# RWKV pairs: value gathers ahead of the key transposes, and most conditioning sums moved beside the first five pairs

## The chip, the core and the metric

The kernel runs on one core of a Trainium2 chip. TensorE (PE) does matmuls and loads its weights in parallel with them (PEld); VectorE (DVE), ScalarE (ACT) and GpSimd (POOL) do elementwise work; SyncE (SP) issues most DMAs, ACT a few. Each engine works through its own instructions strictly in the order that the program fixed, and waits where an operand or a buffer is not there yet. The metric is device time in microseconds (us).

## The reference

Two transformer-like blocks follow each other. Of the first, this case touches the RWKV-7 mixer (16 heads of 64 channels, 256 context and 512 latent tokens, two directions) and the conditioning vectors:

```
shift, scale, gate = split(silu(c) @ w_ada + b_ada, 3)        # 2048 -> 3 * 2048
def step(state, inp):                                         # per head, both directions
    sa = -einsum('bhvk,bhk->bhv', state, kk_t)
    state = state * w_t + sa * b_t + v_t * k_t
    return state, einsum('bhvk,bhk->bhv', state, r_t)
y = groupnorm(o) * gn_g + gn_b; y = (y + bonus) * silu(z)
x = x + gate * (concat([ya, yb]) @ w_out)                     # then rmsnorm, then block two
shift2, scale2, gate2 = split(silu(c_2) @ w_ada_2 + b_ada_2, 3)
```

The scan is computed in chunks of 64 tokens: within a chunk by small triangular solves and matmuls, from chunk to chunk by a chain of states.

## The kernel before

The part that matters lies between 1240 and 2460 us. The 16 heads go two at a time: `for p in range(npairs)` runs eight **pairs** (0 to 7). Each pair does, in this order in the code:

- `rwkv_rest`: Gram matrices `Gr` and the copy `R`, transposes of the keys (`rpt` to `bk`), gathers of values and of A (`rpv`, `rat` to `UV`), products `rgv` to `GS`, and the bonus;
- `rwkv_lanes`: a triangular solve on DVE, 60 dependent operations on `rL` and `rT` (lines 745 and 746) between transposes; here called the **lane solve**;
- `rwkv_keys(p + 1)`: the next pair's decays, keys and Gram matrices `Ga`;
- `rwkv_levels`: the rest of the inverse (`rpy`, `rpx`, `rmx`), alternating PE, ACT and DVE;
- `rwkv_chain`: the **chain** of 12 chunk states. One step is `pU` on PE, `UV` on ACT, `pU` again, and one DVE multiply `GS<-pU,WC` (L1214), 11 of them in a pair;
- `rwkv_out`: group norm, transposes and the gate `z` (tiles `rosq`, `rzt`), stored to `y_scr`.

Beside the pairs run two kinds of filling work. The **projection** `rwkv_proj(p + 2)` makes r, k, v, z of a later pair: 192 matmuls of 128x512 (`mm`, L394) into the PSUM ring `mm[0]` of two buffers, mixed on their way out in a ring `mix` of two SBUF buffers. `Stream` spreads these matmuls over the steps of a pair. After the last projection, the section under `fill out` does the same with the first part of the output projection: it loads 13 tiles `yf` (in `mix`), splits them, and runs 16 groups of 39 matmuls (L1320), each leaving through a tile `pe` (in `mix`).

The **conditioning sums** are `ada_cols`: for 6144 output columns, each `sum over k of cact[k] * w_ada[k]` runs on DVE as a running sum, 16 steps for each block of columns, in tiles `awt` that are loaded one by one:

```
wt = wts(k); SY.dma_start(wt, wsrc(k))
V.scalar_tensor_tensor(wt, wt, cvec[:, k:k + 1], acc, op0=OP.mult, op1=OP.add)
acc = wt
```

At the end of a block, matmuls with a column of ones add over the partitions into a PSUM tile `pm`. Before the change all 12 blocks of 512 columns (192 steps) stand under `fill out`, in a ring of six `awt` buffers. `early = ()` keeps the loop that would place blocks of 256 columns beside the pairs empty.

Two things set the order. A pool's ring hands out buffers in the order of the code: a tile waits until the tile that had its buffer before is released. And a scheduler orders each engine's instructions from its own estimates, with the pairs at high priority, `Stream` and `Beside` as earliest points; this order is then fixed in the program.

Of the kernel before, what the change touches and what calls it, by code (L numbers as in the profile page):

```python
# [10 lines left out]
FT = mybir.dt.float32  # L11
FR = mybir.dt.float32r
AF = mybir.ActivationFunctionType
# [5 lines left out]
P = 128  # L19
D = 2048  # L20
KT = 16
NX = 512
# [182 lines left out]
def build(tc, a, dbg=None):  # L205
# [3 lines left out]
    PE, V, S, G, SY = nc.tensor, nc.vector, nc.scalar, nc.gpsimd, nc.sync  # L209
    root = ExitStack()  # L210
    with root:
# [17 lines left out]
        ident = cc("ident", P)  # L229
# [23 lines left out]
        mm = [actx.enter_context(tile_pool(name="mps", bufs=2, space=PSUM))]  # L253
# [193 lines left out]
        for i in range(4):  # L447
            px, pc = lx[i], lc[i // 2][:, i % 2]
            m = vc("mu", 24 + i)
# [53 lines left out]
        for d in range(2):  # L503
# [7 lines left out]
            Gr, raw = rows[:, 0], rows[:, 1]  # L511
# [417 lines left out]
        def pg_(shape, name):  # L929
            return gps.tile(shape, FT, name=name, tag="g", bufs=2)  # L930
# [40 lines left out]
        def rwkv_out(p, s):  # L971
            mark(f"r{p} out")
            po, bv = s["po"], s["bv"]
            oa = rp.tile([P, NX], FT, name="oa").rearrange("p (m h t) -> p m h t", m=4, h=2)
            oa8 = oa.rearrange("p m h t -> p (m h) t")
            po8 = po.rearrange("p m h t -> p (m h) t")
            mean = rp.tile([P, 8], FT, name="gmean")
            var = rp.tile([P, 8], FT, name="gvar")
            osq = rp.tile([P, NX], FT, name="rosq").rearrange("p (m t) -> p m t", m=8)
            bc8 = lambda t: t.rearrange("p (j o) -> p j o", o=1).to_broadcast([P, 8, 64])  # L980
            V.tensor_reduce(mean, po8, axis=AX.X, op=OP.add)
            V.tensor_scalar(mean, mean, 1.0 / 64, None, op0=OP.mult)
            V.tensor_tensor(oa8, po8, bc8(mean), op=OP.subtract)
            S.activation(osq, oa8, AF.Square)
            V.tensor_reduce(var, osq, axis=AX.X, op=OP.add)
            zt = rp.tile([P, NX], FT, name="rzt", tag="rosq")
            SY.dma_start(zt, mix_scr["z"][p])
            V.tensor_scalar(var, var, 1.0 / 64, 64e-5, op0=OP.mult, op1=OP.add)
            rsqrt_pow(var, var, 8)
            V.tensor_tensor(oa8, oa8, bc8(var), op=OP.mult)  # L990
            pt = cps.tile([P, 4, P], FT, name="rpto", tag="pU")
            for m in range(4):
                PE.transpose(pt[:, m, :], oa[:, m].rearrange("p h t -> p (h t)"), ident)
            yt = oa.rearrange("p m h t -> p (m h t)")
            S.activation(yt, pt.rearrange("p m t -> p (m t)"), AF.Identity, scale=vc("gn", p), bias=vc("gn", 8 + p))
            G.tensor_tensor(yt, yt, bv, op=OP.add)
            G.tensor_tensor(yt, yt, zt, op=OP.mult)
            S.dma_start(y_scr[8 + p], yt)
# [92 lines left out]
        def rwkv_rest(p, s):  # L1091
# [3 lines left out]
            Gr = [rp.tile([P, 8, 2, 64], FT, name="Gr", bufs=2) for d in dirs]  # L1095
            bk = [rp.tile([P, NC, P], FT, name="bk", bufs=2) for d in dirs]
            R = [rp.tile([P, 2, 8, 64], FT, name="R", bufs=2) for d in dirs]
            for d in dirs:
                gram(p, d, Gr[d], BK[d], A[d][:, NC:], 4, 8, ccr(f"rm{d}")[:, 64:])
                for h, hp_ in enumerate(halves):  # L1100
                    S.activation(R[d][64:, h], A[d][hp_, NC:], AF.Copy)
                for c0 in range(0, NC, 4):
                    pt = pg_([P, 4, P], "rpt")
                    for c in range(4):
                        PE.transpose(pt[:, c, :], BK[d][:, c0 + c, :, :].rearrange("p j t -> p (j t)"), ident)
                    S.activation(bk[d][:, c0:c0 + 4, :], pt, AF.Copy)

            UV = rp.tile([P, NC, 2, 2, 64], FT, name="UV")

# [3 lines left out]
            for d in dirs:  # L1113
# [14 lines left out]
                for c0 in range(0, NC, 4):  # L1128
                    i0 = step_chunk[d].index(c0 + (3 if d else 0))
                    pt = gps.tile([P, 4, P], FT, name="rat", tag="l")  # L1130
                    for c in range(4):
                        PE.transpose(pt[0:64, c, :], A[d][:, c0 + c], ident)
                    S.activation(UV[0:64, c0:c0 + 4, d].rearrange("p c h t -> p c (h t)"), pt[0:64], AF.Copy)
                    pt = gps.tile([P, 4, 2, 64], FT, name="rgv", tag="l")
                    for i in range(4):
                        for h in range(2):
                            PE.matmul(pt[halves[h], i, h, :], Ga[64:, d, step_chunk[d][i0 + i], h], UV[64:, i0 + i, d, h, :], start=True, stop=True, skip_group_check=True)
                    for h, hp_ in enumerate(halves):
                        S.activation(GS[0:64, i0:i0 + 4, d, h], pt[hp_, :, h], AF.Copy)

            V.scalar_tensor_tensor(ksum, rr, vc("r_k", p), ksum, op0=OP.mult, op1=OP.mult)
            pb = pg_([P, NX], "rbo")
# [135 lines left out]
                return tc.issue_after(states[min(i, len(states) - 1)])  # L1278

        start = []  # L1280
        early = ()
        for p in range(1, min(2, npairs)):
            rwkv_proj(p, r0, False, pace, tag="mix", bufs=2)
        with tc.high_priority(offset=4000):
# [1 line left out]
        for p in range(npairs):  # L1286
# [8 lines left out]
                now = nxt  # L1295
            beside = Beside()
            for i in range(early[p] if p < len(early) else 0):
                ada_cols(256 * (sum(early[:p]) + i), 256, lambda k: rp.tile([P, 256], FT, name="awt", bufs=4), gps, "l", beside)
            if p + 2 < npairs:
                stream.n = min(stream.n, start[p])  # L1300
                rwkv_proj(p + 2, r0, False, stream, tag="mix", bufs=2)
# [485 lines left out]
```

## Time and profile before

| | |
|---|---|
| time, median of 3 runs | 3392.07 us (3390.76 to 3399.92) |
| the profiled execution: its time, its span | 3378.85 us, 3377.1 us |
| PE, PEld busy | 3093.9 us (92%), 2447.9 us (72%) |
| DVE busy | 2324.4 us (69%) |
| ACT, POOL busy | 1303.7 us (39%), 952.6 us (28%) |
| granted TensorE clock, mean share of full | 0.924 |

Busy shares are means over stages of different limits: matmuls overlap and their ends are modelled, so a PE at 92% is not at its peak, and a DVE at 69% can be the bound of a stage. In rows of instructions the columns are start and duration in us, engine, line, operation, tiles (written <- read) and, in brackets, the engine's idle time just before and what ended it.

### The profile page before, as it was taken

The page shows a single profiled execution, that of the slowest core. Times are in us where ns is not written, and L with a number is a line of the kernel's source. Part 1 is how long each engine was busy: PE and PEld are TensorE (multiplying, and loading weights), DVE is VectorE, ACT ScalarE, POOL GpSimd, SP SyncE. Part 2 cuts the span into 40 slices and gives each one's busy share as a digit, 9 for nine tenths or more (in the row PEclk, how much of TensorE's full clock was granted, in tenths as well). Part 3 has the DMA queues.
Part 4 walks back from the last instruction along what each step waited for, and adds up shares of the span by engine and source line. Part 5 has one row for each costly group of instructions (what it writes and reads, how often), then busy time and mean ns, then how long its engine had stood idle before and what let it go on. Part 6 is the DMA issues. An engine that isn't in the chain of part 4 may idle for free.

```text
span 3377.1 us, 53576 instructions
## 1 busy us (share of the span) xinstructions
PE 3093.9 (92%) x20464; PEld 2447.9 (72%) x20464; DVE 2324.4 (69%) x3996; ACT 1303.7 (39%) x2767; POOL 952.6 (28%) x794
## 2 busy tenths in 40 slices
PE   7798998999898989999999998989978999999996
PEld 4477887788776867677677776667656778877775
DVE  7977678776887254755646637797678997573577
ACT  5133443344333234435344342413233336573423
POOL 3644343344343232233223232523041000002001
PEclk9899999998999877999999978788989999999998
DMA  8522222222222221212112112568653322223764
GB/s 338 190 76 79 79 70 65 71 84 72 67 65 83 90 70 48 64 49 79 56 59 61 51 55 95 180 186 253 197 198 134 114 84 88 85 79 119 261 212 137
DMA packets 206265, 375.13 MB, mean 111 GB/s; under 512 B 21911, under 2 KB 52280, under 8 KB 202680
## 3 DMA queue, kind: packets, MB, share of 16 engines
q1 hardware_dynamic: 196384, 356.07, 32.9%
q10 hardware_dynamic: 9624, 15.64, 1.3%
q8 instruction: 160, 2.62, 0.3%
q14 instruction: 97, 0.79, 0.1%
HBM read 333.75 MB, written 37.88 MB: 110 GB/s over the span
## 4 chain that ended last, share of the span: by engine, by line
PE 55%; DVE 27%; issue 6%; DMA 3%; ACT 2%; POOL 1%; SPq 0%; DVEq 0%; POOLq 0%; ACTq 0%
PE mm L394 24%; PE po L1758 4%; PE mm L1477 4%; DVE L L746 3%; DVE DG L745 3%; PE rpg L1065 3%; DVE awt L1254 2%; DVE rT L745 2%; DVE rL L746 2%; PE pU L93 2%; DVE acc L587 2%; DMA awt<-in_w_ada 2%; DVE uc L1496 2%; PE mm L1320 2%; PE pl L1016 1%
## 5 line engine op out<-in xcount | busy, mean ns | idle before, releaser
L275 POOL TENSOR_TENSOR w_l<-w_f,w_h 128x512 fp32r<-128x512 f32 x380 | 535.8, 1412 | 1036.7 <-ACT w_h L274 962.3
L274 ACT ACTIVATE w_h<-w_f 128x512 fp32r<-128x512 f32 (+2 forms) x688 | 424.4, 618 | 785.4 <-PE mm L394 265.8
L394 PE MATMUL mm<-hxh,w_l 128*128 128x512 f32 x1472 | 621.5, 422 | 15.5 <-POOL w_l L275 10.0
L394 PE MATMUL mm<-hxh,w_h 128*128 128x512 f32 x1472 | 623.0, 423 | 11.9 <-ACT w_h L274 10.7
L394 PE MATMUL mm<-hxl,w_h 128*128 128x512 f32 x1472 | 606.8, 413 | 0.0
L394 PEld LDWEIGHTS mm<-hxh,w_l 128*128 128x128 f32 x1472 | 290.6, 197 | 77.8 <-POOL w_l L275 12.6
L394 PEld LDWEIGHTS mm<-hxh,w_h 128*128 128x128 f32 x1472 | 288.9, 196 | 74.2 <-ACT w_h L274 13.5
L394 PEld LDWEIGHTS mm<-hxl,w_h 128*128 128x128 f32 x1472 | 289.7, 197 | 61.0 <-issue 1.5
L275 DVE TENSOR_TENSOR w_l<-w_f,w_h 128x512 fp32r<-128x512 f32 (+2 forms) x308 | 219.4, 715 | 145.8 <-ACT w_h L274 144.0
L1254 DVE SCALAR_TENSOR_TENSOR awt<-awt,cacts 128x512 f32<-128x512 f32 x180 | 169.3, 940 | 30.0 <-DMA awt<-in_w_ada 19.6
L1496 DVE SCALAR_TENSOR_TENSOR uc<-up,vecs,uc 128x512 f32<-128x512 f32 x240 | 169.4, 747 | 2.2 <-ACT uc L1494 1.0
L394 PE MATMUL mm<-hch,w_l 128*128 128x256 f32 x512 | 153.9, 301 | 1.4 <-POOL w_l L275 1.3
L394 PE MATMUL mm<-hch,w_h 128*128 128x256 f32 x512 | 150.4, 294 | 0.0
L1065 PEld LDWEIGHTS rpg<-A,BK 64*128 64x128 f32 x1280 | 128.6, 217 | 27.7 <-issue 11.4
L394 PE MATMUL mm<-hcl,w_h 128*128 128x256 f32 x512 | 148.3, 290 | 0.0
L1065 PE MATMUL rpg<-A,BK 64*128 64x64 f32 x1280 | 138.1, 307 | 10.5 <-POOL BK L1051 6.8
L745 DVE TENSOR_TENSOR DG<-L 128x30 f32<-128x30 f32 (+14 forms) x240 | 135.2, 563 | 5.3
L746 DVE TENSOR_TENSOR L<-L,DG 128x30 f32<-128x30 f32 (+14 forms) x240 | 134.1, 559 | 5.4
L745 DVE TENSOR_TENSOR rT<-rL 128x30 f32<-128x30 f32 (+14 forms) x240 | 124.4, 518 | 6.7
L1203 ACT ACTIVATE UV<-pU 64x256 f32<-64x256 f32 x96 | 36.2, 377 | 235.0 <-PE pU L1201 223.9
L236 POOL TENSOR_TENSOR cv<-cv,mh 128x4 f32<-128x4 f32 x1 | 1.4, 1435 | 437.5 <-DVE cv L1564 437.5
L746 DVE TENSOR_TENSOR rL<-rL,rT 128x30 f32<-128x30 f32 (+14 forms) x240 | 117.2, 489 | 6.7
(483 smaller groups left out, 6749.3 us busy)
## 6 DMA issues: line engine op xcount, KB each, us to landing
w_f<-in_w_in SPq DMA_DIRECT2D x496, 256.0 KB, 3.0
awt<-in_w_ada SPq DMA_DIRECT2D x192, 256.0 KB, 3.5
wt<-in_w_ada_t SPq DMA_DIRECT2D x20, 1024.0 KB, 6.5
w_f<-in_w_out SPq DMA_DIRECT2D x80, 256.0 KB, 2.9
awt<-in_w_ada_g SPq DMA_DIRECT2D x64, 256.0 KB, 3.6
wk<-in_w_ada_s SPq DMA_DIRECT2D x16, 768.0 KB, 6.0
w_f<-in_w_out_a SPq DMA_DIRECT2D x48, 256.0 KB, 3.6
lth<-lora_scr SPq DMA_DIRECT2D x32, 288.0 KB, 3.1
```

What stands on the lines that cost most here:

```text
L93: i = self.tc.nc.tensor.matmul(out, lhsT, rhs, start=first is None, stop=True, skip_group_check=True)
L274: S.activation(wh, raw, AF.Copy)
L275: lower[0].tensor_tensor(wl, raw, wh, op=OP.subtract)
L394: PE.matmul(po[:, :n], w_[:, k, :], h_, start=(kt == 0 and i == 0), stop=(kt == KT - 1 and i == 2))
L587: V.scalar_tensor_tensor(acc[:, :n], raw[:, j:j + n], cw(j), acc[:, :n], op0=OP.mult, op1=OP.add)
L745: V.tensor_tensor(t, U[:, r, k:k + 1].to_broadcast([n, k, nc_]), U[:, k:k + 1, c].to_broadcast([n, k, nc_]), op=OP.mult)
L746: step = V.tensor_tensor(U[:, r, c], U[:, r, c], t, op=OP.add)
L1065: ticks[p, d, "gram"] = PE.matmul(pg[h][:, c], BK[hp_, c0 + c, :, :], cols[hp_, c], start=True, stop=True, skip_group_check=True).ins
L1254: V.scalar_tensor_tensor(wt, wt, cvec[:, k:k + 1], acc, op0=OP.mult, op1=OP.add)
L1477: PE.matmul(po, w_[:, k, :], h_[kt], start=(kt == 0 and j == 0), stop=(kt == KT - 1 and j == 2))
L1496: V.scalar_tensor_tensor(uc[t], up[:, j:j + NX], cw(j), uc[t], op0=OP.mult, op1=OP.add)
L1758: PE.matmul(po[t], y_[kt][:, cols], w_, start=(kt == 0 and i == 0), stop=(kt == KT - 1 and i == 2))
```

## The change

Four edits. In `rwkv_rest` the Gram matrices, `R` and the key transposes move behind the gathers. The tiles `rosq` and `rzt` of `rwkv_out` move from a buffer of their own into the ring `mix`. `early` becomes `(4, 4, 4, 4, 4)`: 20 blocks of 256 columns (320 steps, five sixths of the columns) move beside pairs 0 to 4, and 2 of the 12 blocks of 512 stay in the fill (`n_early` becomes 10). Those 20 blocks use two `awt` buffers, and their `pm` tiles come from the ring `mm[0]`.

```
-            osq = rp.tile([P, NX], FT, name="rosq").rearrange("p (m t) -> p m t", m=8)
+            osq = r0.tile([P, NX], FT, name="rosq", tag="mix", bufs=2).rearrange("p (m t) -> p m t", m=8)
...
-            zt = rp.tile([P, NX], FT, name="rzt", tag="rosq")
+            zt = r0.tile([P, NX], FT, name="rzt", tag="mix", bufs=2)
...
-            for d in dirs:
-                gram(p, d, Gr[d], BK[d], A[d][:, NC:], 4, 8, ccr(f"rm{d}")[:, 64:])
...
+            for d in dirs:
+                for c0 in range(0, NC, 4):
+                    pt = pg_([P, 4, P], "rpt")
...
+            for d in dirs:
+                gram(p, d, Gr[d], BK[d], A[d][:, NC:], 4, 8, ccr(f"rm{d}")[:, 64:])
+                for h, hp_ in enumerate(halves):
+                    S.activation(R[d][64:, h], A[d][hp_, NC:], AF.Copy)
...
-        early = ()
+        early = (4, 4, 4, 4, 4)
...
-                ada_cols(256 * (sum(early[:p]) + i), 256, lambda k: rp.tile([P, 256], FT, name="awt", bufs=4), gps, "l", beside)
+                ada_cols(256 * (sum(early[:p]) + i), 256, lambda k: rp.tile([P, 256], FT, name="awt", bufs=2), mm[0], "mm", beside)
```

How the fixed order changes, at three places. First VectorE in the chain of pair 3, from its second to its seventh state multiply (`GS<-pU,WC`); before:

```order
L1214 TENSOR_TENSOR GS<-pU,WC 64x256
L1046 SCALAR_TENSOR_TENSOR BK<-lth,k2r 128x12x64
L1039 SCALAR_TENSOR_TENSOR A<-kmix,vecs_r,E 128x12x63
L1214 TENSOR_TENSOR GS<-pU,WC 64x256 x4
L1141 SCALAR_TENSOR_TENSOR ksum<-rmix,vecs_r,ksum 128x512
L1067 TENSOR_TENSOR Ga<-rpg,consts_r 128x8x64 x2
L1080 STREAM_TRANSPOSE rL<-Ga 32x1024 x2
L1067 TENSOR_TENSOR Ga<-rpg,consts_r 128x4x64
L1214 TENSOR_TENSOR GS<-pU,WC 64x256
```

and of the change, in the same chain:

```order
L1215 TENSOR_TENSOR GS<-pU,WC 64x256
L1255 SCALAR_TENSOR_TENSOR awt<-awt,cacts 128x256 x3
L1215 TENSOR_TENSOR GS<-pU,WC 64x256
L1255 SCALAR_TENSOR_TENSOR awt<-awt,cacts 128x256 x2
L425 SCALAR_TENSOR_TENSOR mr<-mm,vecs,mr 128x8x63
L1255 SCALAR_TENSOR_TENSOR awt<-awt,cacts 128x256
L1215 TENSOR_TENSOR GS<-pU,WC 64x256
L1255 SCALAR_TENSOR_TENSOR awt<-awt,cacts 128x256 x3
L1215 TENSOR_TENSOR GS<-pU,WC 64x256
```

Up to three steps of the sums now stand between two multiplies of the chain, and the next pair's lane solve (`rL<-Ga`), which began inside this chain, now begins behind it. From pair 0's second multiply to pair 5's first, all 320 steps stand in VectorE's order: 52 inside the lane solves of pairs 2 to 5 (14, 12, 12, 14), 36 between the ends of these solves and the first multiplies of their chains (8, 10, 10, 8), and 232 elsewhere.

Second TensorE in the chain of pair 7, with output-projection matmuls (`mm`) between the two halves of a step; before:

```order
L1201 MATMUL pU<-GS,Ga 64x64 x4
L1320 MATMUL mm<-hxh_20586,w_h 128x512
L1320 MATMUL mm<-hxh_20586,w_l 128x512
L1320 MATMUL mm<-hxl_20587,w_h 128x512
L1320 MATMUL mm<-hxh_20592,w_h 128x512
L1320 MATMUL mm<-hxh_20592,w_l 128x512
L1320 MATMUL mm<-hxl_20593,w_h 128x512
L1320 MATMUL mm<-hxh_20598,w_h 128x512
L1320 MATMUL mm<-hxh_20598,w_l 128x512
L93 MATMUL pU<-GS,consts 64x256
L93 MATMUL pU<-UV,bk 64x64 x4
```

and of the change, the end of that chain (`rpo` is the output of pair 7, `rpto` its last transposes):

```order
L93 MATMUL pU<-GS,consts 64x256
L93 MATMUL pU<-UV,bk 64x64 x4
L93 MATMUL rpo<-UV,Gr 64x64 x4
L1202 MATMUL pU<-GS,Ga 64x64 x4
L93 MATMUL rpo<-GS,R 64x64 x4
L93 MATMUL rpo<-UV,Gr 64x64 x4
L1321 MATMUL mm<-hxh_21626,w_h 128x512
L1321 MATMUL mm<-hxh_21626,w_l 128x512
L993 MATMUL rpto<-consts,oa 128x128 x4
L1321 MATMUL mm<-hxl_21627,w_h 128x512
```

All 624 matmuls of the partial output projection now stand behind pair 7's last chain step; pairs 6 and 7 have none beside them. Likewise the chains of pairs 0 and 1 have no projection matmuls beside them; the 192 of one projection stand in one block behind chain 1, and those of the others stand in the chains of pairs 2 to 5, some 24 to a step instead of 7 (240 within the ten steps of chain 5).

Third ScalarE, which issues the loads of `yf`, around pair 6's output (`rosq`) before:

```order
L1106 ACTIVATE bk<-rpt 128x512 x3
L1306 DMA yf<-y_scr 128x512
L984 ACTIVATE rosq<-oa 128x512
L1306 DMA yf<-y_scr 128x512
L1309 ACTIVATE hxh_20586<-yf 128x512
```

and in the change around pair 7's, behind the eleven last copies of its chain:

```order
L1204 ACTIVATE UV<-pU 64x256 x11
L984 ACTIVATE rosq<-oa 128x512
L1307 DMA yf<-y_scr 128x512
L1310 ACTIVATE hxh_21626<-yf 128x512
L1307 DMA yf<-y_scr 128x512
L995 ACTIVATE oa<-rpto,vecs_r 128x512
```

The first load of `yf` moved from beside pair 6's end to pair 7's end, since `rosq` and `rzt` of pair 7 now stand ahead of `yf` in the ring `mix`.

## Rows read from the trace of the kernel before

**Rows 1.** Windows by stage: start:end, us, busy by engine, clock, DMA share, GB/s.

```profile
1238.00:1352.80 114.80, 105.28 (x865) 81.39 (x865) 65.90 (x115) 42.44 (x80) 23.99 (x17) 0.70 0.13 38
...
1617.80:1755.10 137.30, 130.43 (x1182) 97.47 (x1181) 81.23 (x133) 56.70 (x106) 41.53 (x30) 0.95 0.20 61
...
2098.00:2304.00 206.00, 176.69 (x1326) 138.85 (x1325) 171.97 (x242) 69.67 (x133) 76.88 (x52) 0.78 0.62 194
2304.00:2461.50 157.50, 147.34 (x1202) 113.06 (x1200) 100.80 (x143) 48.07 (x98) 29.67 (x23) 0.99 0.72 227
2461.50:3377.00 915.50, 849.73 (x3738) 671.59 (x3738) 664.04 (x1039) 383.15 (x761) 92.13 (x70) 0.96 0.42 136
```

**Rows 2.** Groups by form: the sums' step in the fill; a like one of 256 columns.

```profile
L1254 DVE SCALAR_TENSOR_TENSOR awt<-awt,cacts 128x512 f32<-128x512 f32 x180 | 169.3, 940 | 30.0 <-DMA awt<-in_w_ada 19.6 <-DMA awt<-in_w_ada_g 7.0
...
L957 DVE SCALAR_TENSOR_TENSOR k2r<-kmix,vecs_r,rpb 128x256 f32<-128x256 f32 x8 | 3.8, 472 | 4.4 <-PE rpb L955 4.4
```

**Rows 3.** DMA issues, 1490 to 2030 us: tiles, queue, count, size, median us to landing.

```profile
w_f<-in_w_in SPq DMA_DIRECT2D x60, 256.0 KB, 3.3
...
rzt<-mix_z SPq DMA_DIRECT2D x4, 256.0 KB, 2.6
...
wup<-in_w_up SPq DMA_DIRECT2D x8, 48.0 KB, 1.9
```

**Rows 4.** Timeline of DVE and SP: a result, then its store.

```profile
2098.00 0.67 DVE L839 SCALAR_TENSOR_TENSOR mz<-mzth,mm 128x512 f32<-128x512 f32 x1
...
2098.70 0.33 SPq L844 DMA_DIRECT2D mix_z<-mz  x1
```

**Rows 5.** The chain of waits, then DVE's timeline: a load and the step behind it.

```profile
2280.43 4.56 DMA awt<-in_w_ada
...
2285.08 1.20 DVE L1254 SCALAR_TENSOR_TENSOR awt<-awt,cacts 128x512 f32<-128x512 f32 x1 [0.47 <-DMA awt<-in_w_ada]
```

**Rows 6.** Timeline of DVE, late stage: the sums of block two, four buffers.

```profile
3202.31 0.75 DVE L1712 SCALAR_TENSOR_TENSOR awt<-awt,cacts 128x512 f32<-128x512 f32 x1 [0.69 <-DMA awt<-in_w_ada]
3203.85 0.75 DVE L1712 SCALAR_TENSOR_TENSOR awt<-awt,cacts 128x512 f32<-128x512 f32 x1 [0.79 <-DMA awt<-in_w_ada]
```

**Rows 7.** Chain multiplies of pairs 0, 5, 7: durations, first and last start.

```profile
L1214 DVE TENSOR_TENSOR GS<-pU,WC x11: 427/427/428, 1323.2 to 1385.7; 64x256 f32<-64x256 f32 x11
...
L1214 DVE TENSOR_TENSOR GS<-pU,WC x11: 427/428/428, 2024.1 to 2088.5; 64x256 f32<-64x256 f32 x11
...
L1214 DVE TENSOR_TENSOR GS<-pU,WC x11: 427/428/428, 2375.4 to 2433.9; 64x256 f32<-64x256 f32 x11
```

**Rows 8.** Timeline of DVE: two multiplies of chain 7, no `mm` between.

```profile
2402.20 0.43 DVE L1214 TENSOR_TENSOR GS<-pU,WC 64x256 f32<-64x256 f32 x1 [1.11 <-PE pU L93]
...
2405.18 0.43 DVE L1214 TENSOR_TENSOR GS<-pU,WC 64x256 f32<-64x256 f32 x1 [0.51 <-PE pU L93]
```

**Rows 9.** Lane solve of pair 0: first transposes, then the end mark.

```profile
L1080 DVE STREAM_TRANSPOSE rL<-Ga x4: 1889/1896/1899, 1238.0 to 1244.5; 32x1024 f32<-32x1024 f32 x4
L749 DVE MEMSET rL<- x1: 85/85/85, 1276.2 to 1276.2; 128x32 f32 x1
```

**Rows 10.** The chain of waits: matmuls in a row; Gram matmuls of a direction.

```profile
1484.63 1.93 PE rpg L1065 x32
...
2440.15 8.63 PE mm L1320 x36
```

**Rows 11.** Timeline of PE: projection matmuls that start 0.42 us apart.

```profile
1198.28 0.63 PE L394 MATMUL mm<-hxh,w_h 128*128 128x512 f32 x1
1198.70 0.63 PE L394 MATMUL mm<-hxh,w_l 128*128 128x512 f32 x1
```

**Rows 12.** Tile `yf`, 2098 to 2461 us; then PE's first `po` behind the fill.

```profile
L1309 ACT ACTIVATE hxh<-yf x14: 619/631/634, 2103.2 to 2460.9; 128x512 fp32r<-128x512 f32 x14
L1310 POOL TENSOR_TENSOR hxl<-yf,hxh x13: 1266/1708/2777, 2103.9 to 2155.1; 128x512 fp32r<-128x512 f32 x13
...
DMA to landing us min/median/max: 3.0/4.7/6.1
...
2462.46 0.91 PE L1320 MATMUL po<-hxh,w_h 128*128 128x512 f32 x2 [3.34 <-ACT w_h L274]
```

More of the change, by code (lines that the diff above doesn't have):

```diff
@@ L1097, in rwkv_rest @@
             R = [rp.tile([P, 2, 8, 64], FT, name="R", bufs=2) for d in dirs]
-            for d in dirs:
-                gram(p, d, Gr[d], BK[d], A[d][:, NC:], 4, 8, ccr(f"rm{d}")[:, 64:])
[L1100 to L1106, printed above, removed]
             UV = rp.tile([P, NC, 2, 2, 64], FT, name="UV")
@@ L1139, in rwkv_rest @@
                         S.activation(GS[0:64, i0:i0 + 4, d, h], pt[hp_, :, h], AF.Copy)
+            for d in dirs:
+                for c0 in range(0, NC, 4):
+                    pt = pg_([P, 4, P], "rpt")
+                    for c in range(4):
+                        PE.transpose(pt[:, c, :], BK[d][:, c0 + c, :, :].rearrange("p j t -> p (j t)"), ident)
+                    S.activation(bk[d][:, c0:c0 + 4, :], pt, AF.Copy)
+            for d in dirs:
+                gram(p, d, Gr[d], BK[d], A[d][:, NC:], 4, 8, ccr(f"rm{d}")[:, 64:])
+                for h, hp_ in enumerate(halves):
+                    S.activation(R[d][64:, h], A[d][hp_, NC:], AF.Copy)
             V.scalar_tensor_tensor(ksum, rr, vc("r_k", p), ksum, op0=OP.mult, op1=OP.mult)
```

## The prediction

> **What bounds the kernel now.** Read first the windows by stage [rows 1]. One period of the steady pairs (1617.8 to 1755.1) takes 137 us; PE is busy for 130 of it, VectorE (DVE) for 81. So DVE has some 56 us without work in each period. In the fill (2098 to 2461.5) it is the other way: DVE is busy for 273 of 363 us, and 169 of them are the sums' steps [rows 1, 2]. These steps also made DVE wait 30 us, most of it for their own loads. So moving sums from the fill to the pairs moves them to where DVE has room. Whether they can use it depends on what a step waits for, and there the reader should look at the loads, not at DVE.
>
> A step needs its load, and a load needs a free buffer. Block two's sums (far behind, with four buffers) already show steps that DVE waits for: 0.69 and 0.79 us idle ahead of steps 1.54 us apart, each ended by a load [rows 6].
>
> The fixed order decides the rest: every engine takes its instructions in the order shown above, late or not.
>
> **The round trip with two buffers.** Step k reads its own tile and that of step k-1. With two buffers the load for step k+1 takes the buffer of tile k-1, and that is free only when step k has ended. So no load is ever in flight while its predecessor's step still waits: step, issue, load, step, one after the other. The price of one round:
>
> - the step: the trace has no such step of 256 columns; a like operation of that size took 0.472 us [rows 2];
> - step to issue: a result of DVE at 2098.67 let SP issue at 2098.70, 0.03 us [rows 4];
> - the load of 128 KB: between 1.9 us (48 KB) and 2.6 us (256 KB, `rzt`) in the quiet pairs, with 3.3 us for the crowded `w_f` as the far end [rows 3]. I take 2.3, the middle of the first two, since half the loads run while few others do;
> - landing to step: a load issued at 2280.43 took 4.56 us, its step began at 2285.08, 0.09 us later [rows 5].
>
> Sum 2.9 us, bounds 2.5 to 3.9. DVE works for 0.47 of it; 320 rounds are 928 us, but five periods of 137 us are only 685. A period would have to last 64 x 2.9 = 186 us. DVE's room is not what limits.
>
> **First term: from pair 0's first chain multiply to pair 5's.** Before: 1323.2 to 2024.1 [rows 7]. After, by what stands in DVE's order:
>
> - 52 steps inside four lane solves. A solve takes 38.2 us alone [rows 9]; 13 steps between its operations add 13 x 0.47 = 6, and their round trips hide behind five operations each. Four times 44 is 176;
> - 36 steps between a solve's end and its chain. Pair 0 took 47 us there [rows 7, 9], with 33 matmuls of 0.24 us (36 in 8.63 us [rows 10]) that are gone. Nine rounds are 26. I take 35, bounds 26 and 47: four times 35 is 140;
> - the other 232 steps at 2.9: 673. A chain step alone takes 2.98 us [rows 8], so two or three steps between two multiplies set its length, and even 24 projection matmuls beside it (24 x 0.24 + 2.98 = 8.7) only equal three rounds.
>
> Together 989. The start moves forward a little, as 60 projection matmuls (14 us) leave the order ahead of it: taken as 8, so 1315. The end is 2304, **280 us later** than before.
>
> **Second term: the fill that stands behind pair 7.** Before, from pair 5's first multiply to PE's first `po` matmul, 438 us (2024.1 to 2462.5) [rows 7, 12]. After, from the order:
>
> - chain 5 with 240 projection matmuls: 10 x 2.98 + 240 x 0.24 = 88;
> - pair 5's output, 96 more matmuls (23 us) and Gram matrices: 30;
> - pair 6's solve with its last transposes: 41;
> - to its chain: 32 steps of 512 columns at 0.94 [rows 2] and some 34 other DVE operations at 0.43: 45;
> - chain 6, with four to nine operations of the next pair in a step: 10 x 5 = 50; the 39 operations left of pair 7's solve at 0.5: 20;
> - pair 7's levels 35, its chain 10 x 2.98 = 30, its output 5;
> - the 13 loads of `yf` through two buffers: load 4.7, copy 0.63, subtraction 1.71 [rows 12], so 7.0 x 13 / 2 = 46 until the first group can end (bounds 33, with the fastest load and subtraction, and 58);
> - 15 more groups of 39 matmuls at 0.24: 140.
>
> Together 530, **92 us more**. Before, most of these 624 matmuls (150 us of PE) lay between the steps of pairs 6 and 7. The cause is the ring `mix`: `yf` and `pe` now follow pair 7's `rosq` and `rzt` in it. The same ring and the `pm` tiles in `mm[0]` hold each projection back until the sums ahead of it are done; that lies inside the first term, where the sums end last.
>
> **Third term: PE's clock.** Beside pair 0, PE was granted 0.70 of full speed on average, against 0.95 in the steady pairs [rows 1]; in the slow stretches matmuls start 0.42 us apart [rows 11] and not 0.24, so at 1.2 GHz in place of 2.4. PE will have more idle time, with 137 us of the same work in a period of some 190. If a sixth of the six projections' 1152 matmuls run slow, that is 192 x 0.18 = **35 us**; none gives 0, all give 207. On this the Trainium skill speaks against the change: TensorE: Matmul & The Clock Gate, section "Why this matters for your kernels", asks for matmuls without long idle gaps between bursts, since the clock falls in them. By it all would run slow wherever a burst follows a gap, and the sum would be higher by the other 172 us; the row of pair 0, whose average lies between the levels, bears it out in part.
>
> **The other edits.** The gathers ahead of the key transposes: the same instructions, on PE, ACT and DVE, while the lane solve runs for 38 us; they are costed at nothing. Uncovered they would cost some 8 us of Gram matmuls (four times 1.93 [rows 10]) a pair, or save as much if chains begin earlier: 60 us in all at most, either way. The 160 steps of 512 columns that leave the fill (150 us of DVE at 0.94) gain what the second term shows, where other work is then last. Behind the fill nothing changes: 915.5 us [rows 1].
>
> **Sum.** 280 + 92 + 35 = 407 us on the profiled execution's 3378.85 (span 3377.1), which is 3786. That execution lies 0.4% under the median of the runs, 3392; I give 3786.
>
> **The rivals.**
>
> *Faster.* The Trainium skill, Perfetto Trace Analysis, section "Optimization Strategy", holds that interleaving stages with different most-contended engines may gain. As a mechanism here: 64 steps x 0.47 = 30 us fit into the 56 idle us of a period and cost nothing, and the fill, without 150 us of DVE, is left to PE's 324 busy us of 363. That gives 3379 - 39 = 3340. It decides if a round trip is under 137 / 64 = 2.1 us and the output projection still lies beside pairs 6 and 7. No load in rows 3 allows the first, and the order of PE denies the second. Chance 0.02.
>
> *Only the fill moves.* Round trips fit, since the scheduler's order spreads the steps: pairs keep 137 us, and only the second term stays: 3379 + 92 = 3471. It needs the same 2.1 us. Chance 0.06.
>
> *Worse.* Loads of the sums stand in one queue on SP with `w_f`, which waits for split buffers, and PE runs cold. At 3.3 us a load, a round is 3.9: 232 more us; or all projection matmuls slow, 172 more. Beyond 3970 with either and a bit of the other. Chance 0.12.
>
> *The forecast*, the three terms with their bounds, 3620 to 3970: chance 0.79. No change at all (within 0.3%, about what a measurement of this kernel can tell, 10 us) would need gain and loss to cancel: 0.01.
>
> **Range.** Low end: load of 1.9 us (-93), levels at 26 (-36), clock at nothing (-35): 3622. High end: load of 2.7 us (+93) and half the cold matmuls more (+86): 3965. So 3620 to 3970, which leaves out the 0.02, 0.01, 0.06 and 0.12.
>
> **What would show it.** Right: `awt` steps of 256 columns about 2.9 us apart in chain 2 to 4, DVE idle ahead of most of them until a load, one load in flight; the chain multiplies of pair 5 near 2300; DVE's share in a period falling although it has more work; no `mm` of the fill ahead of pair 7's output, then some 190 us of them with PE nearly alone; granted clock under 0.9 in pairs 0 to 4. Wrong: `awt` steps 2.1 us apart or less; loads landing in under 1.7 us; pair 5's chain near 2024. If the end of the pairs is right and the fill is not, the second term was mis-sized; if periods are much over 200 us, it is SP's queue or the clock.

## The result and the profile after

The changed kernel takes 3812.34 us (median of 4 runs, 3809.61 to 3816.66) against 3395.99 for the kernel before on the same chip (4 runs): ratio 1.1223, interval 1.1172 to 1.1274, so slower. The profiled execution took 3811.66 us (span 3809.8) with a mean granted clock of 0.842, against 3378.85 us and 0.924. The prediction was 3786 us with a range of 3620 to 3970.

The 433 us between the two profiled executions split at two landmarks. Pair 5's first chain multiply comes at 2328.3 and not at 2024.1 [rows 7], 304 us later. PE's first `po` matmul comes at 2899.0, 570.7 us behind that multiply and not 438 [rows 7, 12], 132 us more. What stands behind takes 4 us less (910.8 against 914.6, from `po` to the end of the span).

First the windows by stage that answer to [rows 1], with the same columns: pair 0's lane solve and what follows up to the next one, the period of pair 3, chain 5 to pair 7's output, the fill, and what stands behind it.

```profile
1225.40:1333.80 108.40, 88.62 (x740) 69.41 (x740) 69.75 (x123) 36.98 (x71) 15.79 (x11) 0.56 0.09 28
1831.40:2040.40 209.00, 151.61 (x1204) 118.97 (x1203) 110.17 (x200) 56.49 (x106) 42.56 (x30) 0.72 0.26 80
2328.30:2711.00 382.70, 341.80 (x2698) 266.42 (x2698) 190.65 (x311) 118.71 (x226) 84.36 (x61) 0.70 0.22 67
2711.00:2899.00 188.00, 166.40 (x631) 119.98 (x630) 12.06 (x22) 51.87 (x94) 65.78 (x59) 0.90 0.42 127
2899.00:3809.80 910.80, 846.93 (x3739) 669.60 (x3738) 663.03 (x1039) 381.62 (x757) 88.84 (x67) 0.97 0.41 134
```

A period grew from 137 to 209 us. DVE got more work in it (110 us, it was 81), yet its share fell from 59% to 53%: it waits. On what, the groups of DVE's instructions by form say, from 1225 to 2330 us (busy, mean ns, idle time ahead and what ended it), and beside them the loads from 1490 to 2030 us:

```profile
L1255 DVE SCALAR_TENSOR_TENSOR awt<-awt,cacts 128x256 f32<-128x256 f32 x300 | 167.2, 557 | 369.7 <-DMA awt<-in_w_ada 224.1 <-DMA awt<-in_w_ada_g 144.0
```

```profile
awt<-in_w_ada SPq DMA_DIRECT2D x100, 128.0 KB, 2.1
```

370 us of DVE's time went by ahead of 300 steps, nearly all of it until a load landed. The chain that ended last shows one round after the other, between pair 3's lane solve and its chain:

```profile
1899.95 0.49 DVE awt L1255
1900.46 2.14 DMA awt<-in_w_ada
1902.60 0.03 issue
1902.65 0.04 issue
1902.70 0.50 DVE awt L1255
1903.21 2.16 DMA awt<-in_w_ada
```

Step, load, step: 1902.70 - 1899.95 = 2.75 us a round, with nothing else in it. That is the predicted loop; its load is a bit shorter than the 2.3 us that were taken. DVE's timeline in chain 3 shows who stands behind it:

```profile
1923.38 0.48 DVE L1255 SCALAR_TENSOR_TENSOR awt<-awt,cacts 128x256 f32<-128x256 f32 x1 [2.26 <-DMA awt<-in_w_ada]
1926.09 1.35 DVE L1255 SCALAR_TENSOR_TENSOR awt<-awt,cacts 128x256 f32<-128x256 f32 x1 [2.22 <-DMA awt<-in_w_ada]
1927.47 0.43 DVE L1215 TENSOR_TENSOR GS<-pU,WC 64x256 f32<-64x256 f32 x1
```

The chain's multiply at 1927.47 has no idle time of its own: when the two steps ahead of it, which waited for their loads, were through, its operand was there.

The chains of pairs 0, 5 and 7 (answer to [rows 7]), and two multiplies of chain 7 (answer to [rows 8]):

```profile
L1215 DVE TENSOR_TENSOR GS<-pU,WC x11: 427/428/428, 1304.3 to 1369.7; 64x256 f32<-64x256 f32 x11
...
L1215 DVE TENSOR_TENSOR GS<-pU,WC x11: 427/428/429, 2328.3 to 2427.7; 64x256 f32<-64x256 f32 x11
...
L1215 DVE TENSOR_TENSOR GS<-pU,WC x11: 427/427/428, 2654.5 to 2699.4; 64x256 f32<-64x256 f32 x11
```

```profile
2677.80 0.43 DVE L1215 TENSOR_TENSOR GS<-pU,WC 64x256 f32<-64x256 f32 x1 [3.90 <-PE pU L93]
2682.12 0.43 DVE L1215 TENSOR_TENSOR GS<-pU,WC 64x256 f32<-64x256 f32 x1 [3.90 <-PE pU L93]
```

Chain 7 stands alone, with no `mm` in it, and nine of its ten steps take 4.33 us, not the 2.98 of [rows 8]. The multiply waits 3.90 us for PE. The windows of chains 5, 6 and 7 show the clock:

```profile
2328.30:2427.70 99.40, 99.40 (x673) 74.33 (x673) 25.44 (x38) 34.76 (x63) 39.79 (x31) 1.00 0.30 89
2536.90:2601.40 64.50, 61.51 (x423) 45.90 (x424) 30.64 (x54) 11.05 (x24) 8.32 (x7) 0.50 0.00 1
2654.50:2699.40 44.90, 40.93 (x323) 29.77 (x324) 5.53 (x13) 4.53 (x12) 0.00 (x0) 0.50 0.00 1
```

Chain 5, with 263 `mm` beside it, kept PE busy throughout and was granted the full clock; chains 6 and 7, with none, got 0.50, which is the lower level (1.2 GHz). The windows of pair 3 show the same, PE's work in all and then its `mm` alone (busy and number, clock), for the lane solve, from there to the chain, and the chain:

```profile
1831.40:1877.30 45.90, 30.69 (x249) 26.22 (x248) 40.85 (x81) 13.63 (x29) 0.00 (x0) 0.65 0.15 45
1877.30:1906.00 28.70, 17.25 (x276) 15.93 (x278) 12.70 (x27) 7.01 (x12) 0.00 (x0) 0.50 0.15 45
1906.00:2005.80 99.80, 88.74 (x604) 66.24 (x602) 37.01 (x66) 24.42 (x45) 28.73 (x20) 0.89 0.36 110
```

```profile
1831.40:1877.30 45.90, 0.00 (x0) 0.65 0.15 45
1877.30:1906.00 28.70, 0.00 (x0) 0.50 0.15 45
1906.00:2005.80 99.80, 51.91 (x192) 0.89 0.36 110
```

All 192 matmuls of a projection stand in the chain, none in the other two stages, and there PE's clock is granted at 0.65 and 0.50. In the kernel before the same three stages of the same pair had 81, 70 and 78 of them and a clock of 0.93, 0.94 and 0.89:

```profile
1617.80:1666.60 48.80, 23.55 (x81) 0.93 0.14 44
1666.60:1725.40 58.80, 20.98 (x70) 0.94 0.22 65
1725.40:1787.80 62.40, 25.98 (x78) 0.89 0.17 52
```

### The profile page after: what moved, and what is told of

It is laid out like the page before. It is cut to its first block, busy times and chain, and to the rows that moved or that the text cites. A ratio compares the mean times of both kernels' runs of the same rounds, so it can differ in the third digit from the quotient of the medians.

```text
span 3809.8 us, 54144 instructions
## 1 busy us (share of the span) xinstructions
PE 3252.7 (85%) x20464; PEld 2597.0 (68%) x20464; DVE 2326.5 (61%) x4166; ACT 1303.0 (34%) x2767; POOL 933.5 (25%) x794
## 4 chain that ended last, share of the span: by engine, by line
PE 43%; DVE 28%; DMA 14%; issue 5%; POOL 2%; ACT 2%; DVEq 0%; SPq 0%; POOLq 0%; ACTq 0%
PE mm L394 18%; DMA awt<-in_w_ada 8%; DMA awt<-in_w_ada_g 4%; PE po L1759 4%; DVE awt L1255 4%; PE mm L1478 3%; DVE DG L745 3%; DVE L L746 3%; PE pU L93 2%; DVE rL L746 2%; DVE rT L745 2%; DVE acc L587 2%; DVE rL L1080 2%; PE rpg L1065 2%; POOL w_l L275 1%
## 5 line engine op out<-in xcount | busy, mean ns | idle before, releaser
L275 POOL TENSOR_TENSOR w_l<-w_f,w_h 128x512 fp32r<-128x512 f32 x380 | 521.0, 1374 | 1282.3 <-ACT w_h L274 1229.2
L394 PE MATMUL mm<-hxh,w_l 128*128 128x512 f32 x1472 | 613.0, 416 | 10.6 <-POOL w_l L275 5.6
L394 PE MATMUL mm<-hxh,w_h 128*128 128x512 f32 x1472 | 610.5, 415 | 13.3 <-ACT w_h L274 11.8
L394 PE MATMUL mm<-hxl,w_h 128*128 128x512 f32 x1472 | 597.7, 406 | 0.0
L1255 DVE SCALAR_TENSOR_TENSOR awt<-awt,cacts 128x256 f32<-128x256 f32 (+1 forms) x330 | 192.8, 584 | 374.9 <-DMA awt<-in_w_ada 228.8
L1065 PE MATMUL rpg<-A,BK 64*128 64x64 f32 x1280 | 189.5, 384 | 115.9 <-DVE Ga L1067 52.5
L1065 PEld LDWEIGHTS rpg<-A,BK 64*128 64x128 f32 x1280 | 178.9, 291 | 127.8 <-DVE Ga L1067 54.9
L1215 DVE TENSOR_TENSOR GS<-pU,WC 64x256 f32<-64x256 f32 x88 | 37.6, 428 | 142.5 <-PE pU L93 129.9
L1202 PE MATMUL pU<-GS,Ga 128*64 128x64 f32 (+1 forms) x768 | 94.9, 286 | 28.4 <-DVE GS L1215 23.0
L1202 PEld LDWEIGHTS pU<-GS,Ga 128*64 128x64 f32 (+1 forms) x768 | 75.9, 188 | 60.0 <-DVE GS L1215 34.5
## 6 DMA issues: line engine op xcount, KB each, us to landing
wt<-in_w_ada_t SPq DMA_DIRECT2D x20, 1024.0 KB, 6.6
```

Source lines behind the costliest of these rows:

```text
L275: lower[0].tensor_tensor(wl, raw, wh, op=OP.subtract)
L394: PE.matmul(po[:, :n], w_[:, k, :], h_, start=(kt == 0 and i == 0), stop=(kt == KT - 1 and i == 2))
L1065: ticks[p, d, "gram"] = PE.matmul(pg[h][:, c], BK[hp_, c0 + c, :, :], cols[hp_, c], start=True, stop=True, skip_group_check=True).ins
L1202: step = PE.matmul(pU[0:64, d, h], Ga[ks, d, step_chunk[d][i], h], GS[ks, i, d, h], start=True, stop=True, skip_group_check=True)
```

## The experiments

All times are medians, ratios are to the kernel before on the same chip with their interval. "Pairs" is the time from pair 0's first chain multiply to pair 5's, "fill" from there to the first `po`, both from the profiled execution, and the clock is PE's mean granted clock in "pairs". "Idle" is the part of "pairs" in which PE ran nothing, "no `mm`" the part in which it ran other matmuls and no `mm` (its busy time less that of its `mm`), both in us. There are some 4930 of these other matmuls in "pairs" in each run (4884 to 5084).

| run | time, us | ratio | pairs | clock | idle | no `mm` | fill |
|---|---|---|---|---|---|---|---|
| before | 3388 to 3407 | 1 | 700.9 | 0.92 | 33 | 373 | 438.4 |
| changed | 3812.34 | 1.1223 (1.1172 to 1.1274) | 1024.0 | 0.67 | 282 | 526 | 570.7 |
| x1_one_load | 3579.3 | 1.0539 (1.051 to 1.0569) | 815.8 | 0.75 | 80 | 492 | 546.3 |
| x2_sums_in_l | 3980.83 | 1.1728 (1.1688 to 1.1767) | 1245.7 | 0.64 | 409 | 546 | 498.8 |
| x3_four_small | 3738.93 | 1.1009 (1.0982 to 1.1036) | 946.4 | 0.69 | 217 | 516 | 574.5 |
| x4_rosq_t3 | 3731.74 | 1.0988 (1.0962 to 1.1015) | 1029.5 | 0.67 | 300 | 521 | 482.4 |
| x6_half | 3605.06 | 1.0622 (1.0569 to 1.0675) | 828.8 | 0.75 | 106 | 476 | 565.5 |
| e_mix | 3608.03 | 1.0634 (1.0573 to 1.0695) | 784.2 | 0.76 | 42 | 473 | 596.1 |
| e_gather | 3413.96 | 1.0051 (1.0024 to 1.0079) | 737.2 | 0.86 | 43 | 408 | 433.1 |
| x7_small_t3 | 3652.31 | 1.0762 (1.0709 to 1.0816) | 939.8 | 0.70 | 230 | 502 | 481.9 |
| x8_one_load_t3 | 3497.88 | 1.0284 (1.0239 to 1.033) | 824.7 | 0.75 | 100 | 482 | 457.6 |
| x9_half_t3 | 3568.94 | 1.0491 (1.0451 to 1.0532) | 875.3 | 0.72 | 128 | 503 | 475.5 |
| x10_small_early | 3508.4 | 1.0322 (1.028 to 1.0364) | 830.3 | 0.76 | 112 | 474 | 452.8 |
| x12_one_step_t3 | 3495.57 | 1.0316 (1.0244 to 1.0388) | 863.7 | 0.78 | 79 | 493 | 407.4 |

The columns "idle" and "no `mm`" come from such rows, here of the kernel before and of the changed one (PE's work in all, then its `mm`):

```profile
1323.20:2024.10 700.90, 667.73 (x5893) 497.30 (x5895) 401.51 (x654) 289.60 (x541) 213.55 (x155) 0.92 0.20 60
1323.20:2024.10 700.90, 294.60 (x961) 0.92 0.20 60
...
1304.30:2328.30 1024.00, 742.47 (x5723) 586.46 (x5725) 525.08 (x968) 262.22 (x497) 181.39 (x132) 0.67 0.25 75
1304.30:2328.30 1024.00, 216.36 (x793) 0.67 0.25 75
```

**Are the loads the pace?** One load for each block, all DVE operations kept (lines of the new branch):

```
+            if once:
+                wt, acc = wts(0), wts(1)
+                SY.dma_start(wt, wsrc(0))
...
+                            V.scalar_tensor_tensor(acc, wt, cvec[:, k:k + 1], acc, op0=OP.mult, op1=OP.add)
```

> Each 256-column block loads one tile, into one of the two buffers, and its 16 steps all read that tile and add into the other buffer: 20 loads instead of 320, the same 320 DVE operations. What it leaves out: 15 of the 16 weight tiles of those blocks, so five sixths of the conditioning columns aren't the reference's sums. Theory (a round trip step, issue, load, step sets the pace): the steps no longer wait, the time from pair 0's first chain multiply to pair 5's falls from 1024 us to some 720 to 780, the granted clock in these periods goes back over 0.85, and the time falls by 230 to 300 us, to 3510 to 3580; the fill stays behind pair 7, so it isn't back at 3396. Rival one (DVE's work or its order, not the loads): within 60 us of the changed kernel. Rival two (pm tiles in the ring of the projection hold it back): a fall of less than 120 us.

The groups of DVE by form, 1304 to 2260 us:

```profile
L1256 DVE SCALAR_TENSOR_TENSOR awt<-awt,cacts 128x256 f32<-128x256 f32 x300 | 187.2, 624 | 4.3
```

The same 300 steps, 4.3 us idle and not 370. The time falls by 233 us, 208 of them in the pairs, where PE's idle time falls by 201. That is the theory's side and both rivals fall. But its numbers for the pairs (720 to 780) and the clock (over 0.85) were missed: 815.8 and 0.75. Some 115 us of the pairs' loss have another cause. The scheduler's order changed with this edit too (chain 3 has 95 `mm` beside it and not 192), so the 208 us are those of the loads and of that order together.

Four buffers of half the size instead of two, twice the steps:

```
-        early = (4, 4, 4, 4, 4)
+        early = (8, 8, 8, 8, 8)
...
-                ada_cols(256 * (sum(early[:p]) + i), 256, lambda k: rp.tile([P, 256], FT, name="awt", bufs=2), mm[0], "mm", beside)
+                ada_cols(128 * (sum(early[:p]) + i), 128, lambda k: rp.tile([P, 128], FT, name="awt", bufs=4), mm[0], "mm", beside)
...
-            na = n_early = sum(early) // 2
+            na = n_early = sum(early) // 4
```

> The same columns in the same 2 KB of a partition, but as four buffers of 128 columns: 640 steps instead of 320, up to three loads in flight instead of one. DVE gets more work, not less. Theory: a round is shared by three loads, so steps come 0.8 to 1.1 us apart in place of 2.74; 640 of them want 510 to 700 us, about what five undisturbed pairs last; from pair 0's chain to pair 5's 720 to 800 us instead of 1024, the time 3510 to 3620. Rival one (DVE or its order is the limit): more operations, so no faster than 3812, rather slower. Rival two (SP's queue, in which each load is issued and may stand behind another that waits): 640 issues instead of 320 make it slower, over 3850.

Groups by form, 1304 to 2260 us:

```profile
L1255 DVE SCALAR_TENSOR_TENSOR awt<-awt,cacts 128x128 f32<-128x128 f32 x600 | 257.8, 430 | 167.1 <-DMA awt<-in_w_ada_g 80.5 <-DMA awt<-in_w_ada 75.6
```

More DVE work, less waiting (167 us) and 73 us less time: the direction is the theory's, and neither rival's. The size was missed: 3739, not 3510 to 3620. Steps came 0.87 us apart (median), as expected, but the pairs lost only 78 of their 1024 us: DVE idled some 203 us less ahead of the steps and worked some 91 us more in them, and the clock stayed at 0.69.

**Is it pm in the projection's ring?**

```
-... name="awt", bufs=2), mm[0], "mm", beside)
+... name="awt", bufs=2), gps, "l", beside)
```

> The changed kernel with the pm tiles of the 20 moved blocks in the ring gps "l", as the line before had it, instead of mm[0], so that no projection matmul waits for a sum. Theory (the pace of 2.74 us a step sets pairs 0 to 4 whatever the projection does): pair 5's first chain multiply stays within 40 us of 2328, the time within 40 us of 3812, PE's granted clock perhaps a bit higher since the projection can spread. Rival (the sums' place in mm[0] holds the projection back, and that makes the periods long): a fall of 100 us or more, with pair 5's chain before 2230.

It became 169 us slower, which neither expected. DVE's groups between pair 1's lane solve and its chain (1441 to 1511 us) show what happened:

```profile
L1255 DVE SCALAR_TENSOR_TENSOR awt<-awt,cacts 128x256 f32<-128x256 f32 x24 | 13.8, 573 | 48.7 <-DMA awt<-in_w_ada_g 48.7
```

Here a run of steps stands between a solve and its chain and DVE idles 48.7 us in it, while PE is busy for 12 of 68 us in that stretch. In the changed kernel many rounds lie beside the projection matmuls of a chain; here they stand on the pair's own path. The place of the steps in the order decides how much of a round is paid. The fall that the rival forecast did not come. But the projection stands elsewhere too in this order (all 192 of pair 3 between its solve and its chain), so the run does not say what `mm[0]` alone costs.

**The fill.** The ring of `rosq` and `rzt`, in the changed kernel and then alone in the kernel before:

```
-            osq = r0.tile([P, NX], FT, name="rosq", tag="mix", bufs=2).rearrange("p (m t) -> p m t", m=8)
+            osq = t3("rosq", NX).rearrange("p (m t) -> p m t", m=8)
...
-            zt = r0.tile([P, NX], FT, name="rzt", tag="mix", bufs=2)
+            zt = t3("rzt", NX)
```

> The changed kernel with rosq and rzt in the ring t3 of six buffers instead of mix, so that the tiles yf and pe need not follow pair 7's in mix. Theory of the second term: the 624 matmuls of the partial output projection lie beside pairs 6 and 7 again, PE's first po matmul comes some 440 us behind pair 5's first chain multiply and not 571, the time falls by 90 to 130 us, to 3680 to 3720; the periods of pairs 0 to 4 and pair 5's chain near 2328 are unchanged. Rival (the fill is late because the sums end late, or because of the clock, and not because of the ring): within 30 us of 3812.

The fill falls from 570.7 to 482.4 us and the pairs stay (1029.5): the ring is the cause of 88 of the 132 us; the other 44 stay open. The time, 3732, is 12 us over the expected range. Loads and first copies of `yf`, in the changed kernel and with the ring t3:

```profile
L1307 ACTq DMA_DIRECT2D yf<-y_scr x16: 326/326/445, 2705.5 to 2741.2; - x16
```

```profile
L1307 ACTq DMA_DIRECT2D yf<-y_scr x16: 326/326/447, 2500.3 to 2812.8; - x16
```

With the ring mix all come behind pair 7's chain (2699.4), in 36 us; with t3 13 of the 16 are issued ahead of chain 6's first multiply (2555.3), and chains 6 and 7 have 195 and 124 `mm` beside them again.

The edit alone, on the kernel before:

```
-            osq = rp.tile([P, NX], FT, name="rosq").rearrange("p (m t) -> p m t", m=8)
+            osq = r0.tile([P, NX], FT, name="rosq", tag="mix", bufs=2).rearrange("p (m t) -> p m t", m=8)
...
-            zt = rp.tile([P, NX], FT, name="rzt", tag="rosq")
+            zt = r0.tile([P, NX], FT, name="rzt", tag="mix", bufs=2)
```

> The kernel before with only rosq and rzt moved into the ring mix; sums all in the fill, gathers as before. Theory of the second term (the ring alone puts the partial output projection behind pair 7): pair 5's first chain multiply unchanged at about 2024, no mm of the fill ahead of pair 7's output, PE's first po 70 to 130 us later, time 3470 to 3530. Rival (the ring matters only because the sums come late): within 20 us of 3396.

3608 us, twice the loss that was expected. The fill is 158 us longer, and the pairs, which were expected to stay, 83 us, with no sum beside them. The `mm` of pair 3 in its lane solve, from there to the chain, and the chain:

```profile
1643.80:1688.00 44.20, 2.31 (x11) 0.58 0.05 16
1688.00:1789.40 101.40, 47.84 (x172) 0.83 0.23 71
1789.40:1844.50 55.10, 5.25 (x21) 0.67 0.07 22
```

The projection is bunched between solve and chain and no longer lies evenly beside the three stages; in the other two the clock is 0.58 and 0.67, and the later chain steps take 4.33 us each. These two stages are none the longer for it (44 and 55 us, 49 and 62 before): the loss stands in the middle one, 101 us and not 59, into which the projection moved. In the table PE's time without `mm` is 100 us longer, its idle time 9.

Both repairs together:

> The changed kernel with both repairs: the moved blocks as 128 columns in four buffers, and rosq and rzt in the ring t3. If the two losses are apart (pace of the pairs, place of the fill), their gains add: 3812 - 73 - 80 = 3659, within 20 us. If they are one (a later end of the pairs pushes the fill, or the shorter periods leave the fill less to lie beside), it is over 3690 or under 3630. Not faster than the kernel before, since the steps' own DVE time and the lower granted clock remain.

(The edits of the runs x3_four_small and x4_rosq_t3.) 3652 us: the gains add, as the expectation has it for two separate losses.

**The gathers alone** (the edit of the change, on the kernel before):

> The kernel before with only the order in rwkv_rest changed: gathers of values and of A, then key transposes, then Gram matrices. Costed at nothing with 60 us to either side in the prediction. Theory: within 15 us of 3396 (the lane solve of 38 us covers both orders). Rival one (chains begin earlier): 20 to 60 us faster. Rival two (Gram matrices and R uncovered, or PE emptier ahead of the lanes): 20 to 60 us slower.

3414 us, 0.5% slower, at the edge of what was expected. The pairs are 36 us longer at a clock of 0.86, the fill 5 shorter; but the profiled execution before lies 20 us under that kernel's median on this chip (3399), so part of the 36 us may be the spread between executions.

**Room, or a price for each step?**

```
-        early = (4, 4, 4, 4, 4)
+        early = (2, 2, 2, 2, 2)
```

> The changed kernel with early = (2, 2, 2, 2, 2): 10 blocks of 256 columns (160 steps, 32 to a pair) beside pairs 0 to 4 and 7 blocks of 512 in the fill; buffers and rings as in the changed kernel. Theory A (room, the picture of the prediction): a round costs only where more rounds stand in a period than fit; 32 of 2.74 us are 88 us, they fit into a period of 137, so from pair 0's chain to pair 5's it is 700 to 770 us and the time, with the fill still behind pair 7, 3510 to 3570. Theory B (price for each step: the runs with one load, with small buffers and the changed kernel itself lie near 0.70 of the steps' busy time plus 0.55 of the idle time ahead of them, over 701 us): 160 steps are 78 us busy and 194 idle, 54 + 107, so some 860 us from chain to chain and a time of 3630 to 3680.

> The run with half of the moved blocks (32 rounds to a pair, two buffers of 256 columns) and rosq and rzt in the ring t3. With the ring mix it lost 128 us between pair 0's chain and pair 5's. Theory A with C (rounds that fit a period are free, the 128 us were mostly the ring): 701 to 760 us, time 3400 to 3480. Theory B (a price for each step whatever the room): 830 to 860 us, time 3530 to 3580.

(x9_half_t3 is x6_half with the ring t3.) The first, 3605, lies between the two theories, its pairs (828.8) nearer to B; the second, 3569 with pairs of 875.3, is in B's range of time and 15 us over its pairs. So theory A, by which rounds are free where they fit into a period, falls. That the rounds themselves are the cost does not follow: x8_one_load_t3 below loses 124 us in the pairs with hardly a wait for a load.

Small steps on the kernel before, its gathers kept:

```
-        early = ()
+        early = (4, 4, 4, 4, 4)
...
-... 256, lambda k: rp.tile([P, 256], FT, name="awt", bufs=4), gps, "l", beside)
+... 128, lambda k: rp.tile([P, 128], FT, name="awt", bufs=4), mm[0], "mm", beside)
...
-            na = n_early = sum(early) // 2
+            na = n_early = sum(early) // 4
```

(and `rosq`, `rzt` in t3)

> The kernel before, its gather order kept, with 20 blocks of 128 columns (320 steps, 64 to a pair) beside pairs 0 to 4 in four buffers, rosq and rzt in the ring t3, 7 blocks of 512 left in the fill. Rounds of 0.87 us are 56 us of a period of 137, DVE's extra work 23 us of it. Theory: pairs keep 137 to 145 us (700 to 740 from chain to chain), the fill, which PE bounds, gains little: 3370 to 3440, so no clear gain over the kernel before. Rival (a price for each step: 0.7 of 113 us busy and 0.55 of 91 idle): 130 us more, 3500 to 3550.

3508 us, pairs 129 us longer than before: the rival's number. This is the fastest version here that computes all sums with some of them beside the pairs, and it is 3% slower than the kernel before.

**What is the price?** x1_one_load with the ring t3, then that with one of 16 steps:

> The run with one load to a block (15 of 16 weight tiles of the 20 moved blocks left out, the DVE operations all kept) and rosq and rzt in the ring t3. It asks what the 115 us were that pairs 0 to 5 still lost without load waits. Theory C (the ring mix: with it alone and no sums beside the pairs they lost 83 us): from pair 0's chain to pair 5's 700 to 745 us, time 3400 to 3460, so the steps' own 155 us of DVE are hidden. Theory D (the steps' DVE time on the pairs' path, 0.7 of it, or pm in the projection's ring): 800 to 830 us again, time 3480 to 3530.

```
-                for k in range(KT):
+                for k in range(1):
```

> The run with one load to a block and rosq and rzt in t3, and of the 16 steps of each moved block only the first (20 steps on DVE instead of 320; 15 of 16 products of those columns are left out); loads, pm matmuls in the ring mm[0], gather order and ring t3 as there. It asks what the 124 us were that remained without load waits and without the ring mix. Theory D (the steps' own time on DVE, 155 us, lies mostly on the pairs' path): from pair 0's chain to pair 5's 700 to 750 us, time 3380 to 3440. Theory E (pm in the projection's ring, or the new order of the gathers, bunches the projection and leaves PE at the lower clock): 790 to 830 us, time 3470 to 3510.

x8_one_load_t3 took 3498 us, pairs 824.7: theory D's numbers, and C falls. Then x12_one_step_t3 left 300 steps out and took 3496 us (ratio 1.0316, against 1.0284), so D falls too: without the steps' own 155 us of DVE the loss is as large. B's formula had fitted, but not for its reason. Theory E has the time right, but not the pairs (790 to 830): they took 863.7 us, with some 95 more `mm` between the landmarks than before, and the fill is shorter for it. `mm` in the three stages of pair 3 of x12_one_step_t3,

```profile
1678.70:1727.80 49.10, 32.55 (x126) 0.97 0.23 70
1727.80:1827.80 100.00, 13.26 (x44) 0.68 0.15 46
1827.80:1923.60 95.80, 47.77 (x169) 0.87 0.18 53
```

and its middle stage takes 100 us at a clock of 0.68, not 58.8 at 0.94. It is not the same work: 783 matmuls stand in it (the row at the end of this document), and before

```profile
1666.60:1725.40 58.80, 55.36 (x622) 43.54 (x622) 23.88 (x40) 30.98 (x58) 17.87 (x13) 0.94 0.22 65
```

only 622, with more `mm` among them. The table has the remaining loss in one figure: in x1, x8, x10, x12 and e_mix PE's time without `mm` is 100 to 120 us over the 373 of before, for the same number of such matmuls. While they ran, 2083 (e_mix) and 2259 (x12_one_step_t3) of them had the lower clock, 474 before. That the remaining loss goes with a bunched projection and a lower clock is shown. How it divides between the clock and the lost overlap with `mm` is not. What bunches it in this run (`pm` in `mm[0]`, the gathers, the ring t3, or the scheduler's places for the blocks) is not settled: x10_small_early keeps the old gathers and loses the same, and the ring t3 was not run alone.

## Why the prediction was right, step by step

**The round trip** was right as a mechanism, and slightly too dear: 2.74 us is the median distance of two steps (2.9 taken). One load was in flight at a time: two were for 5 of the 1024 us, as far as the trace tells when they landed. The faster rival's condition, under 2.1 us, was not met.

**First term.** 989 us against 1024. In pairs 2 to 5 the lane solves took 47.2, 45.9, 44.2 and 46.1 us (44 taken), solve to chain 31.9, 28.7, 27.6 and 32.7 (35 taken); the other 232 steps took the rest, some 3.1 us each and not 2.9: the median round was shorter than 2.9, but one in five took over 3.5 us, most likely in line behind other work. The start was 1304.3 (1315). That one load to a block gave back 208 of these 323 us shows the loads; the 115 that stayed were no part of the term's reasoning. In PE's time the 323 are 248 us more idle, 153 more on other matmuls without `mm`, and 78 less on `mm`; with one load to a block 201 of the idle us are gone and 119 of the others stay. That 989 came so near is in part luck: each round was charged in full, while by that run only 208 of the 370 us that DVE idled ahead of the steps were paid, and the 115 us of another cause fill the place of the rest.

**Second term** was mis-sized: 92 predicted, 132 measured. Chains 5, 6 and 7 took 99, 65 and 45 us (88, 50 and 30), and that is the whole difference of 41, the other items cancel. In chains 6 and 7, at a clock of 0.50, ten steps of 4.33 us where 2.98 was taken are 13.5 of the 15 us each. Chain 5 is another matter: PE was busy for all of its 99 us at the full clock, with 263 `mm` and not 240. The `mm` groups took 10.2 us each (39 matmuls at 0.24: 9.4), the last `yf` was issued 36 us behind the first, and the first group ended 41 us behind it (46; the bounds given for that item, 33 and 58, come to 32 and 62 from its rows). The ring as the cause is shown for 88 us.

**Third term** was mis-sized, and in the wrong place: 35 us for slow projection matmuls. PE was busy for 742 us of the pairs and 668 before, with 170 fewer instructions, so at least 75 us. None of it fell on the projection: between the landmarks 75 of 793 `mm` had the lower clock while they ran, 101 of 960 before. It fell on the others, on which chain steps and levels wait: 3235 of 4927 had it, 474 of 4933 before. A chain step's 40 matmuls took 4.32 us at 0.50 and 2.98 at 1.00 (last section), 34 ns more for each; 2760 of them are some 93 us, an estimate from these counts and rows, of the 153 us above. The row that was read for the clock [rows 11] is a projection's; [rows 8] was taken as if a chain step had one length, and its 2.98 us is the shortest of the 80 steps of the kernel before. The rule of the Trainium skill (TensorE: Matmul & The Clock Gate, "Why this matters for your kernels"), weighed there with 172 us more, points the right way: the stages without `mm` ran at 0.50 to 0.65; the 172 us themselves, for all projection matmuls, did not come. Idle gaps alone do not explain the rest: in chain 7 PE was busy for 41 of 45 us and granted 0.50.

**The other edits.** "Costed at nothing", 60 us either way, held for the gathers (+0.5%). For the ring mix the prediction saw only the fill: alone it costs 209 us, 83 of them in the pairs. In the changed kernel taking it back gains only 81, all in the fill; that the sums hold the projection there anyhow is the likely reason, not shown.

**Only the fill moves** (3471) fell: the pairs took 1024 us and not 701. **Worse** did not come: `w_f` landed in 3.4 us, the sums' loads in 2.1, and SP issued 298 of these 318 loads within 0.2 us (median 0.03) of the last step's end, so its queue hardly slowed them. In sum 304 + 132 - 4 = 432 us stand against 280 + 92 + 35 = 407; the clock's part is inside the first two.

## What to carry to other kernels

A running sum in two buffers is a loop of step, issue and load, and its price depends on what stands behind it in the engine's order; count rounds, not busy time. Before giving matmul-rich filler work another buffer ring, ask where its instructions will then stand: an even spread kept the clock up for the small dependent matmuls here, and one ring changed alone cost 209 us. When a formula fits four runs, still take away the thing that it names: the steps' busy time fitted, and without it the loss was as large.

## What was not expected of the hardware

The same chain step took 2.98 us [rows 8] or 4.33 us. The first row is of that step of the kernel before, the second of a step of chain 7 in the changed one; neither has an `mm` in it, and the clock is 1.00 in one and 0.50 in the other:

```profile
2402.20:2405.18 2.98, 2.60 (x41) 1.86 (x35) 2.44 (x4) 0.38 (x1) 0.00 (x0) 1.00 0.82 217
...
2677.80:2682.12 4.32, 4.22 (x40) 3.13 (x38) 0.42 (x1) 0.38 (x1) 0.00 (x0) 0.50 0.00 0
```

In a stretch of x12_one_step_t3 PE was busy for 87 of 100 us and yet granted 0.68:

```profile
1727.80:1827.80 100.00, 87.24 (x783) 69.10 (x781) 30.54 (x55) 38.85 (x72) 16.54 (x13) 0.68 0.15 46
```

A busy PE was thus no sign of a high clock. Halving a load from 128 KB to 64 KB shortened it from 2.1 to 1.9 us only, so the size of a load hardly mattered for the round.
